# A hybrid decoder step: both roundings of a seam's bank ahead of its remainders, and a scheduler priority on one read of the decode's gates

## The chip, the cores and the metric

One core of a Trainium2 chip runs the kernel. The core has five engines with an instruction stream each: TensorE (PE, matmuls and transposes; its weight loads are shown apart as PEld), VectorE (DVE), ScalarE (ACT), GpSimd (POOL, which here mostly issues gathers) and SyncE (SP, which issues plain transfers). The metric is the device time of one execution in microseconds; the times shown are medians over several runs.

## The reference

One layer of a decoder, applied to a prompt of 1024 rows and to 8 decode sequences of one new row and 8192 cached rows each. All in fp32, D_MODEL 1024, D_FF 2816, 8 attention heads of 64, a paged key/value cache.

```
q, k, v, logf, u, z = mixer_inputs(rmsnorm(xp, g_mix), w_in, b_f, g_sgu_v)
xp = xp + merge_heads(fox_prompt(q, k, v, logf), sgu_prompt(u, z, w_s, b_s), g_att_out, g_sgu_out, w_o)
mk, mv = memory_kv(mem_prompt, g_mem, w_ck, w_cv)
xp = xp + cross_attend(rmsnorm(xp, g_cross), mk, mv, w_cq, w_co)
f, conv = conv_ffn(rmsnorm(xp, g_ffn), zeros, w_up, conv_w, conv_b, w_down)
xp = xp + f
...
def fox_attend(q, k, v, cq, ck, qpos, kpos):
    s = jnp.einsum('bqhd,bkhd->bhqk', q, k).astype(jnp.float32) * (ATT_HEAD_DIM ** -0.5)
    s = s + (cq... - ck...)
    p = jax.nn.softmax(where(kpos <= qpos, s, -inf), axis=-1)
    return jnp.einsum('bhqk,bkhd->bqhd', p, v)
```

The decode sequences go through the same steps with keys and values gathered by a page table; their attention over 8192 rows carries a forget gate, whose cumulated sum is subtracted from the scores.

## The kernel before

**Precision.** TensorE multiplies fp32 operands that have been rounded to a shorter form (fp32r). To keep fp32 accuracy each operand is split in two: the rounded value and the remainder. A product is then three matmuls: `gemm3` issues rounded x rounded (L272), rounded x remainder (L273) and remainder x rounded (L274); `gemm3_late` issues the same three in two sweeps (L280, L281, then L284). The helper `split` does the rounding on ScalarE (L235, or L238 where a gain is multiplied in) and the remainder on VectorE (L236, or L239). The remainder reads the rounded value, so L239 always waits for its L238. Weights are fetched in 128x1024 pieces by SyncE (names wr) and split as they come (wh and wl).

**Stages.** The prompt runs through input projection, attention, gating and output projection, and then, in two halves of 512 rows ("first half", "second half"), through cross-attention and the gated feed-forward network (FFN). The decode's attention runs beside all of that: its keys are gathered by GpSimd in pieces of 128x2048 (L1428), multiplied by the query on VectorE (L1444) and summed per head (L1448); after 16 pieces a softmax follows (L1460 and L1462, a transpose L1468, L1471 to L1474, L1481, the subtraction L1483, the exponent L1484 on ScalarE, the sum L1485); its values are gathered (L1489) into the same kind of buffer (kv) and multiplied on TensorE (L1495). The decode's instructions are put in as background work between the prompt's: `behind(e)` ties one to the newest instruction of engine e.

**The seams.** Between one stage of a half and the next stands a norm. `out_proj` adds to the rows (L1015), squares them (L230) and computes a factor per block of rows (L1031 on ScalarE, L1032 on GpSimd, a power); L1037 scales blocks 0 and 1, L1044 (ScalarE) and L1045 (VectorE) scale blocks 2 and 3 (y2, y3). `norm_T` then transposes the rows on TensorE (L1124), four 128x128 pieces to a bank of PSUM, with two row blocks (t0 = 0, then 2) and four banks for each; a bank holds two quarters of 128x256. For each quarter in turn it calls `split` with the norm's gain: ScalarE rounds (L238), VectorE takes the remainder (L239). `fill` (L1102) puts filler products ahead of the late transposes. `first` issues the products of the next stage's first outputs that need nothing more. `norm_T` runs four times: the cross seam and the FFN seam of the first half (about 521 to 548 us and 685 to 706 us in the profile), and those of the second (about 1154 to 1180 us and 1317 to 1337 us).

**The gates.** `gates` runs once for each of the 8 decode sequences. A small matmul (L1418) puts the sums of the gates into PSUM (ms), and one VectorE instruction (L1420) reads it and writes the decay per position (dec), which the softmax's first instruction (L1460) uses.

**What sets the order.** The program's text gives each instruction and its priority. The order on each engine is made at build time by a scheduler that simulates a timeline: at each point it takes the ready instruction of the best priority, by its own estimate of durations. Within `tc.high_priority()` an instruction gets precedence; `tc.issue_after(x)` makes it wait for x to be issued. At run time each engine then takes its instructions strictly in that order, so an instruction that waits holds up everything behind it. A change to a few lines can thus move instructions far away.

## Time and profile before

| | before |
|---|---|
| median of 3 runs | 1794.42 us (1788.66, 1794.93, 1794.42) |
| the profiled execution | 1793.69 us |
| its span, first to last instruction | 1791.7 us |
| mean granted TensorE clock | 0.993 |
| groups of L238 at the seams, 128x256 | 64 instructions, mean 475 to 477 ns |
| groups of L239 at the seams, 128x256 | 64 instructions, mean 473 ns |
| L1420 | 8 instructions, mean 1062 ns |

The profile is that of one execution. Its tables give the busy time of each engine; where an engine stood idle, the timeline shows in brackets how long, and the instruction whose end released it. "u" in these views is any operand buffer of the prompt (a rounded value, a remainder or a scaled row block), "ba" and "bb" are banks of PSUM, "kv" a decode buffer, "s" the decode's scores.

### The profile page before, as it was taken

To read this page: it belongs to the slowest core of one execution; us is meant where nothing else is said; L and a number is where in the kernel's file an instruction comes from. 1 tells how busy PE (TensorE), PEld (TensorE's weight loads), DVE (VectorE), ACT (ScalarE), POOL (GpSimd) and SP (SyncE) were. 2 spreads that over 40 slices of the span, in tenths; PEclk is the share of its full clock that TensorE was granted. 3 is DMA by queue.
4 is the path that set the end of the run, shared out by engine and by line. 5 is a ranking of instruction groups with operands and counts; after the bars stand their busy time and mean duration, and the time that the engine had idled before them with its cause. 6 is when DMAs were issued, how large, how long until landed. Compare 5 with 4: busy or idle time off the path is not lost.

```text
span 1791.7 us, 25124 instructions
## 1 busy us (share of the span) xinstructions
PE 1735.9 (97%) x9653; PEld 1285.7 (72%) x9653; DVE 1399.9 (78%) x1733; ACT 733.5 (41%) x1374; POOL 488.3 (27%) x461
## 2 busy tenths in 40 slices
PE   8999999889999999999999999999999999999997
PEld 5787777655677666767777777766666778768875
DVE  4689658989788986989999999898885549855344
ACT  6332355566643635333333244335353233333232
POOL 1252234443222332333322223433322112102110
PEclk9999999999999999999999999999999999999999
DMA  8786798777697975779788788988879587568982
GB/s 291 297 304 226 294 334 319 259 264 244 254 403 279 363 299 224 282 285 345 290 301 313 291 317 311 376 306 346 320 280 350 214 306 249 191 260 297 359 310 80
DMA packets 157074, 521.06 MB, mean 291 GB/s; under 512 B 20874, under 2 KB 40842, under 8 KB 124186
## 3 DMA queue, kind: packets, MB, share of 16 engines
q0 software_dynamic: 57168, 341.14, 50.0%
q1 hardware_dynamic: 92874, 165.73, 26.5%
q10 hardware_dynamic: 6912, 12.59, 1.9%
q8 instruction: 76, 1.25, 0.3%
q14 instruction: 44, 0.36, 0.1%
HBM read 495.47 MB, written 23.93 MB: 290 GB/s over the span
## 4 chain that ended last, share of the span: by engine, by line
PE 53%; issue 9%; DMA 8%; DVE 6%; ACT 2%; POOL 2%; POOLq 0%; DVEq 0%; ACTq 0%; SPq 0%
DMA kv<-cache_v,io 6%; PE ba L272 6%; PE ba L274 6%; PE ba L273 6%; PE dv L1495 4%; PE bb L272 3%; PE bb L273 3%; PE bb L274 3%; PE ba L1063 1%; DVE s L1448 1%; PE ba L1064 1%; PE ba L1065 1%; PE dv L331 1%; DMA kv<-cache_k,io 1%; PE dv L1774 1%
## 5 line engine op out<-in xcount | busy, mean ns | idle before, releaser
L235 ACT ACTIVATE wh<-wr 128x1024 fp32r<-128x1024 f32 (+2 forms) x220 | 228.6, 1044 | 443.3 <-PE ba L273 142.3
L236 DVE TENSOR_TENSOR wl<-wr,wh 128x1024 fp32r<-128x1024 f32 (+2 forms) x220 | 262.7, 1200 | 165.1 <-PE ba L274 57.4
L1428 POOL DMA_INDIRECT kv<-cache_k,io x128 | 186.9, 1460 | 606.8 <-DVE s L1448 327.2
L1444 DVE TENSOR_TENSOR kv<-kv,d 128x1024 f32<-128x1024 f32 (+1 forms) x156 | 258.0, 1681 | 32.6 <-DMA kv<-cache_k,io 32.6
L1448 DVE TENSOR_REDUCE s<-kv 128x16 f32<-128x1024 f32 (+1 forms) x156 | 258.4, 1672 | 0.0
L1489 POOL DMA_INDIRECT kv<-cache_v,io x128 | 160.8, 1256 | 239.4 <-PE dv L1495 155.2
L272 PE MATMUL ba<-u,wh 128*128 128x512 f32 x528 | 209.3, 397 | 0.0
L274 PE MATMUL ba<-u,wl 128*128 128x512 f32 x528 | 209.0, 396 | 0.0
L273 PE MATMUL ba<-u,wh 128*128 128x512 f32 x528 | 208.5, 395 | 0.5 <-DVE u L239 0.5
L272 PE MATMUL ba<-wh,u 128*128 128x512 f32 (+1 forms) x495 | 186.1, 379 | 0.9 <-ACT u L235 0.9
L273 PE MATMUL ba<-wl,u 128*128 128x512 f32 (+1 forms) x495 | 185.1, 375 | 1.3 <-DVE wl L236 1.3
L274 PE MATMUL ba<-wh,u 128*128 128x512 f32 (+1 forms) x495 | 183.4, 375 | 0.0
L1495 PE MATMUL dv<-kv,s 128*32 128x512 f32 x1024 | 127.1, 598 | 1.6 <-DMA kv<-cache_v,io 1.6
L274 PEld LDWEIGHTS ba<-u,wl 128*128 128x128 f32 x528 | 99.2, 188 | 29.0 <-issue 6.5
L272 PEld LDWEIGHTS ba<-u,wh 128*128 128x128 f32 x528 | 99.3, 188 | 26.4 <-issue 4.8
L273 PEld LDWEIGHTS ba<-u,wh 128*128 128x128 f32 x528 | 99.2, 188 | 25.2 <-issue 2.3
L272 PEld LDWEIGHTS ba<-wh,u 128*128 128x128 f32 x495 | 93.0, 188 | 25.0 <-issue 6.5
L272 PE MATMUL bb<-u,wh 128*128 128x512 f32 x272 | 108.7, 400 | 0.0
L274 PE MATMUL bb<-u,wl 128*128 128x512 f32 x272 | 108.0, 398 | 0.0
L273 PE MATMUL bb<-u,wh 128*128 128x512 f32 x272 | 107.9, 397 | 0.0
L273 PEld LDWEIGHTS ba<-wl,u 128*128 128x128 f32 x495 | 93.0, 188 | 20.1 <-DVE wl L236 1.9
L274 PEld LDWEIGHTS ba<-wh,u 128*128 128x128 f32 x495 | 92.9, 188 | 19.5 <-issue 1.6
(454 smaller groups left out, 3310.6 us busy)
## 6 DMA issues: line engine op xcount, KB each, us to landing
wr<-w_up SPq DMA_DIRECT2D x88, 512.0 KB
kv<-w_up POOLq DMA_DIRECT2D x22, 1024.0 KB
wr<-w_down SPq DMA_DIRECT2D x40, 512.0 KB
kv<-w_down POOLq DMA_DIRECT2D x11, 1024.0 KB
wr<-w_in SPq DMA_DIRECT2D x16, 512.0 KB
wr<-w_o SPq DMA_DIRECT2D x16, 512.0 KB
wr<-w_cq SPq DMA_DIRECT2D x16, 512.0 KB
wr<-w_co SPq DMA_DIRECT2D x16, 512.0 KB
```

Of the source, the lines that this page charges most:

```text
L235: nc.scalar.activation(h, src, AF.Copy)
L236: nc.vector.tensor_tensor(l, src, h.bitcast(F32), op=ALU.subtract)
L272: mmul(out, sh, mh, start=(i == 0), stop=False)
L273: mmul(out, sh, ml, start=False, stop=False)
L274: mmul(out, sl, mh, start=False, stop=(i == n - 1))
L331: mmul(ps[32 * j : 32 * j + 32, :w], xT[:, k, :] if nk == 8 else xT[:, k * 8 : k * 8 + 32], raw[:, q, j * w : (j + 1) * w], start=(k == 0) ...
L1063: mmul(pss[i], mh[k][:, tb], wh, start=(k == korder[0]), stop=False)
L1428: nc.gpsimd.indirect_dma_start(kv, None, a["cache_k"], off(kidx[:, b, ch : ch + 1]))
L1444: nc.vector.tensor_tensor(kvv[:, i : i + m, :], kvv[:, i : i + m, :], qb.unsqueeze(1).broadcast_to((P, m, 512)), op=ALU.mult)
L1448: nc.vector.tensor_reduce(s[:, ch * 4 + i : ch * 4 + i + m, :].rearrange("p k h -> p (k h)"), kvv[:, i : i + m, :].rearrange("p k (h d) -> ...
L1489: nc.gpsimd.indirect_dma_start(kv, None, a["cache_v"], off(kidx[:, b, ch : ch + 1]))
L1495: mmul(dv[32 * j : 32 * j + 32, :], s[:, ch * 4 : ch * 4 + 4, :].rearrange("p k h -> p (k h)"), kvv[:, j, :], start=(ch == 1), stop=(ch == ...
```

## The change

Two edits. In `norm_T` the call of `split` for each quarter becomes: both roundings of a bank first (the new L1130), then both remainders (the new L1132). The arithmetic is that of `split` with a gain. In `gates` the one VectorE read is put under `tc.high_priority()`. No instruction is added or left out; from the new lines on, numbers are 5 higher, and 6 higher behind L1420.

```diff
-                    for q in range(2):
-                        k = kk + q
-                        split(tr[:, q * 256 : (q + 1) * 256], hs[k][:, c], ls[k][:, c], scale=gp[:, g0 + k : g0 + k + 1])
+                    gain = [gp[:, g0 + k : g0 + k + 1] for k in (kk, kk + 1)]
+                    src = [tr[:, q * 256 : (q + 1) * 256] for q in range(2)]
+                    for q in range(2):
+                        nc.scalar.activation(hs[kk + q][:, c], src[q], AF.Copy, scale=gain[q])
+                    for q in range(2):
+                        nc.vector.scalar_tensor_tensor(
+                            ls[kk + q][:, c], src[q], gain[q], hs[kk + q][:, c].bitcast(F32), op0=ALU.mult, op1=ALU.subtract
+                        )
...
-            nc.vector.tensor_tensor(
-                dt_, ps[:, :8].unsqueeze(1).broadcast_to((P, 64, 8)), A.rearrange("p (h k) -> p k h", k=64), op=ALU.subtract
-            )
+            with tc.high_priority():
+                nc.vector.tensor_tensor(
+                    dt_, ps[:, :8].unsqueeze(1).broadcast_to((P, 64, 8)), A.rearrange("p (h k) -> p k h", k=64), op=ALU.subtract
+                )
```

The order on the engines is the same up to about 520 us of the profile of before and again from about 1463 us. Between them 237 pieces differ on TensorE, and there are moves on all engines. The priority alone accounts for one of them: VectorE's read dec_1245 (near 678 us) steps in between the two halves of a multiply that it followed. Three places follow.

ScalarE at the FFN seam of the first half, before. u_1266, u_1269, u_1272 and u_1275 are the rounded banks 1 to 4 of the first two row blocks, two quarters each; u_982 is row block 2, u_1278 is y2.

```order
L238 ACTIVATE u_1266_6305<-bb_1268_6307,gp_82 128x256
L238 ACTIVATE u_1269_6316<-ba_1271_6318,gp_82 128x256
L238 ACTIVATE u_1272_6327<-ba_1274_6329,gp_82 128x256
L235 ACTIVATE wh_1311_6576<-wr_1309_6573 128x1024
L238 ACTIVATE u_1266_6305<-bb_1268_6307,gp_82 128x256
L238 ACTIVATE u_1269_6316<-ba_1271_6318,gp_82 128x256
L235 ACTIVATE wh_1318_6630<-wr_1316_6627 128x1024
L238 ACTIVATE u_1272_6327<-ba_1274_6329,gp_82 128x256
L230 ACTIVATE junk_1255_6274,sqx_1193_5897<-u_982_4762 128x512
L238 ACTIVATE u_1275_6338<-bb_1277_6340,gp_82 128x256
L1031 ACTIVATE fac2_1257_6279<-sqx_1193_5897,part_1194_5898 128x1
L1044 ACTIVATE u_1278_6373<-u_982_4762,fac2_1257_6279 128x512 x2
```

The same place in the change:

```order
L1130 ACTIVATE u_1266_6305<-bb_1268_6307,gp_82 128x256 x2
L1130 ACTIVATE u_1269_6316<-ba_1271_6318,gp_82 128x256 x2
L1130 ACTIVATE u_1272_6327<-ba_1274_6329,gp_82 128x256 x2
L235 ACTIVATE wh_1311_6576<-wr_1309_6573 128x1024
L235 ACTIVATE wh_1318_6630<-wr_1316_6627 128x1024
L1130 ACTIVATE u_1275_6338<-bb_1277_6340,gp_82 128x256 x2
L230 ACTIVATE junk_1255_6274,sqx_1193_5897<-u_982_4762 128x512
L1031 ACTIVATE fac2_1257_6279<-sqx_1193_5897,part_1194_5898 128x1
L1044 ACTIVATE u_1278_6373<-u_982_4762,fac2_1257_6279 128x512 x2
```

The second roundings of banks 1 to 3 have moved ahead of the weights' roundings; both of bank 4 now stand ahead of the square L230, where before the first stood behind it and the second behind L1044 (beyond the rows shown).

VectorE at the cross seam of the second half, before. u_1874, u_1877, u_1880 and u_1883 are the remainders of banks 1 to 4 of the last two row blocks; kv_1816 is a decode piece.

```order
L1448 TENSOR_REDUCE s_1633_8615<-kv_1815_9600 128x16 x2
L239 SCALAR_TENSOR_TENSOR u_1874_9910<-ba_1885_9977,gp_82,u_1873_9909 128x256
L1444 TENSOR_TENSOR kv_1816_9650<-kv_1816_9650,d2_1632_8613 128x1024 x2
L239 SCALAR_TENSOR_TENSOR u_1877_9921<-bb_1886_9986,gp_82,u_1876_9920 128x256
L1020 TENSOR_TENSOR rq0_1889_10037<-sqx_1787_9485 128x4
L239 SCALAR_TENSOR_TENSOR u_1880_9932<-ba_1887_9995,gp_82,u_1879_9931 128x256
L239 SCALAR_TENSOR_TENSOR u_1883_9943<-ba_1888_10004,gp_82,u_1882_9942 128x256
L239 SCALAR_TENSOR_TENSOR u_1874_9910<-ba_1885_9977,gp_82,u_1873_9909 128x256
L1448 TENSOR_REDUCE s_1633_8615<-kv_1816_9650 128x16 x2
```

The same place in the change:

```order
L1450 TENSOR_TENSOR kv_1816_9650<-kv_1816_9650,d2_1632_8613 128x1024 x2
L1015 TENSOR_TENSOR u_1804_9517<-ba_1850_9801,u_1804_9517 128x512
L1454 TENSOR_REDUCE s_1633_8615<-kv_1815_9600 128x16
L1132 SCALAR_TENSOR_TENSOR u_1874_9910<-ba_1885_9977,gp_82,u_1873_9909 128x256 x2
L1132 SCALAR_TENSOR_TENSOR u_1877_9921<-bb_1886_9986,gp_82,u_1876_9920 128x256 x2
L1454 TENSOR_REDUCE s_1633_8615<-kv_1816_9650 128x16 x2
L1132 SCALAR_TENSOR_TENSOR u_1880_9932<-ba_1887_9995,gp_82,u_1879_9931 128x256 x2
L1132 SCALAR_TENSOR_TENSOR u_1883_9943<-ba_1888_10004,gp_82,u_1882_9942 128x256 x2
```

Both multiplies of kv_1816 have moved ahead of the first remainder of bank 1 and ahead of the addition L1015; its sums stand between banks 2 and 3.

TensorE in the FFN of the first half, before. The two L1495 rows (4 matmuls each) are the first pair of V products of the decode sequence whose scores are s_1022; ba, bb, wh and u are the FFN's.

```order
L272 MATMUL bb_1367_6943<-u_1269_6316,wh_1366_6940 128x512
L1495 MATMUL dv_1322_6668<-kv_1324_6670,s_1022_5011 32x512 x4
L1495 MATMUL dv_1322_6668<-kv_1323_6669,s_1022_5011 32x512 x4
L273 MATMUL bb_1367_6943<-u_1270_6317,wh_1366_6940 128x512
L274 MATMUL bb_1367_6943<-u_1269_6316,wl_1365_6939 128x512
```

In the change:

```order
L272 MATMUL ba_1385_7075<-wh_1377_6994,u_1330_6711 128x512
L273 MATMUL ba_1385_7075<-wl_1376_6993,u_1330_6711 128x512
L1501 MATMUL dv_1322_6668<-kv_1324_6670,s_1022_5011 32x512 x4
L1501 MATMUL dv_1322_6668<-kv_1323_6669,s_1022_5011 32x512 x4
L272 MATMUL ba_1398_7121<-wh_1391_7106,u_1298_6520 128x512
```

The pair stands 57 rows later, in the down projection instead of the up projection. The second pair (kv_1349 and kv_1350) moves 41 rows, from 3126 to 3167 of TensorE's order, so 27 rows lie between the starts of the pairs where 43 lay. On ScalarE the exponent of s_1022 moves from ahead of the rounding of wh_1391 to behind that of wh_1397, and on VectorE the subtraction L1483 and the sum L1485 of s_1022 stand behind several remainders of weights that they preceded.

## The prediction

> **What bounds the kernel now.** I read the page first (busy shares, slices, chain), then who waits for the split's instructions, then the timelines of the engines at the four seams, and last the stretch where the order moves most.
>
> ```profile
> PE 1735.9 (97%) x9653; PEld 1285.7 (72%) x9653; DVE 1399.9 (78%) x1733; ACT 733.5 (41%) x1374; POOL 488.3 (27%) x461
> PE   8999999889999999999999999999999999999997
> DVE  4689658989788986989999999898885549855344
> PE 53%; issue 9%; DMA 8%; DVE 6%; ACT 2%; POOL 2%; POOLq 0%; DVEq 0%; ACTq 0%; SPq 0%
> ```
>
> The span is 1791.7 us, so TensorE is idle for 1791.7 - 1735.9 = 55.8 us in all. No reordering that leaves the matmuls as they are can win more than that, and a seam can only give back the wait that stands in front of a matmul there. VectorE is the second bound: its slices 17 to 25 of 40 (717 to 1120 us) stand at 8 and 9. What is late in that stretch has little room to catch up.
>
> Who waited for the rounding (the call in L1129, whose two instructions are L238 on ScalarE and L239 on VectorE):
>
> ```profile
>   DVE u L239: 13.2, 8
>   PEld ba L280: 3.1, 5
>   PEld bb L280: 2.2, 2
>   PE bb L280: 1.7, 1
>   PE ba L280: 1.2, 3
> ```
>
> VectorE lost 13.2 us to it and TensorE 1.7 + 1.2 = 2.9; the weight loads' idle time lies beside TensorE's. A saving on VectorE is a saving of the kernel only where TensorE waits behind it.
>
> **The change, part by part.** It adds and removes no instruction: 64 roundings and 64 remainders of 128x256 remain, at 475 and 473 ns each by their groups. What changes is (a) the order written in a bank, (b) a priority on eight reads, and (c) what the scheduler makes of both on every engine from about 520 us on.
>
> *The priority (b).*
>
> ```profile
> L1420 DVE TENSOR_TENSOR dec<-ms,d x8: 1021/1063/1084, 150.4 to 1286.2; 128x512 f32<-128x512 f32 x8
>   PE ms L852: 2.7, 1
> ```
>
> Only one of the eight reads moves: dec_1245 steps ahead of one half of a kv multiply near 678 us. The one time that TensorE waited for such a read (2.7 us) is at 315 us, ahead of the first moved instruction. Nobody waits at 678; the multiply behind it (128x1024, 1218 ns by its group) is 1.06 us later on VectorE. If TensorE did wait for what that multiply feeds, it would cost 1.06 us; by the row I take 0.
>
> *Cross seam of the first half.* Here TensorE has no idle time to return:
>
> ```profile
> 521.00:548.00 27.00, 27.00 (x163) 20.64 (x163) 26.10 (x37) 12.89 (x27) 5.18 (x5) 1.00 0.94 344
> ```
>
> Gain 0. Loss: other decode work covers the remainders; without that cover one bank would cost two remainders, 0.95 us. I take 0.
>
> *FFN seam of the first half.*
>
> ```profile
> 694.00 0.39 PE L280 MATMUL ba<-u,wh 128*128 128x256 f32 x1 [0.32 <-ACT u L238]
> 695.51 0.38 PE L280 MATMUL ba<-u,wh 128*128 128x256 f32 x1 [0.57 <-DVE u L239]
> 697.71 0.33 PE L1124 MATMUL bb<-cp,u 128*128 128x128 f32 x1 [1.70 <-ACT u L1044]
> 698.68 0.39 PE L280 MATMUL ba<-u,wh 128*128 128x256 f32 x1 [0.64 <-ACT u L238]
> 704.00 0.27 PE L1124 MATMUL ba<-cp,u 128*128 128x128 f32 x1
> 696.32 1.33 ACT L1044 ACTIVATE u<-u,fac 128x512 f32<-128x512 f32 x2 [0.68 <-POOL fac L1032]
> 698.17 0.45 ACT L238 ACTIVATE u<-bb,gp 128x256 fp32r<-128x256 f32 x1
> 698.66 0.48 DVE L239 SCALAR_TENSOR_TENSOR u<-bb,gp,u 128x256 fp32r<-128x256 f32 x1 [2.69 <-ACT u L238]
> 699.47 0.88 DVE L1045 TENSOR_SCALAR u<-u,fac 128x512 f32<-128x512 f32 x2 [0.33 <-POOL fac L1032]
> ```
>
> The fourth bank's second rounding stood behind the scaling of y2 (L1044) and came at 698.17; now it follows the first at about 695.4. The waits of 0.32, 0.57 and 0.64 go. In exchange two roundings stand ahead of the square (L230) that starts the chain square, factor, power on GpSimd, scaling: L1044 begins about 1.0 us later (697.4) and y3 (L1045) at 699.47 + 1.0 = 700.5. TensorE now has the bank's products behind it and waits for y3 instead; the last transpose follows the end of y3's second half (700.5 + 0.88 = 701.4) by about eight transposes of 0.12 us, so it ends near 702.4 where it began at 704.00 before. That gives 1.6 us. Bounds: nothing, if y3 is later still; 3.2 us, the sum of the four waits, if the scaling is not delayed. I take -1.6.
>
> The clock is part of that place:
>
> ```profile
> 694.00:698.00 4.00, 1.73 (x9) 1.14 (x9) 1.97 (x5) 2.89 (x7) 0.57 (x1) 1.00 1.00 420
> 699.40:703.00 3.60, 3.60 (x20) 3.60 (x19) 2.41 (x7) 0.75 (x3) 1.04 (x2) 0.53 0.67 278
> ```
>
> After 4 us in which TensorE was busy for 1.73, it ran at 0.53 for 3.6 us, which costs 3.60 x 0.47 = 1.7 us. Those filler products (L1102) lie ahead of the transposes that set the end, so the dip is inside the 1.6 us, not added to it. The Trainium skill, "TensorE: Matmul & The Clock Gate", section "Part 1: The HAM clock gate (the "warmup" mystery)", says that the clock falls to half after an idle window of about 3.4 us. The longest gap here is 1.70 us, so the trace disagrees: scattered waits were enough. By the page no dip would come with or without the change and the seam's sum would hold only the waits; by the row a denser seam may keep the clock, and a longer wait for y3 may lose it.
>
> *Decode work behind that seam (706 to 810 us).* This is the largest move. The softmax of the running decode sequence (subtraction L1483, exponent L1484, sum L1485) comes 12 to 20 us later in VectorE's and ScalarE's order, weight remainders (L236) come earlier, and the first pair of V products on s_1022 stands 57 TensorE rows later.
>
> ```profile
> L1495 PE MATMUL dv<-kv,s x32: 592/592/617, 769.4 to 783.6; 128*32 128x512 f32 x32
> 778.73 0.39 PE L273 MATMUL ba<-wl,u 128*128 128x512 f32 x1
> 780.57 0.40 PE L273 MATMUL bb<-wl,u 128*128 128x512 f32 x1
> 782.27 1.06 PE L1495 MATMUL dv<-kv,s 128*32 128x512 f32 x8 [1.31 <-DMA kv<-cache_v,io]
> 770.78 0.94 POOL L1489 DMA_INDIRECT kv<-cache_v,io  x1 [11.38 <-PE dv L1495]
> 772.02 4.86 POOL L1489 DMA_INDIRECT kv<-cache_v,io  x1 [0.30 <-issue]
> 777.18 2.14 POOL L1428 DMA_INDIRECT kv<-cache_k,io  x1 [0.30 <-issue]
> 787.47 2.29 DVE L1444 TENSOR_TENSOR kv<-kv,d 128x2048 f32<-128x2048 f32 x1 [4.25 <-DMA kv<-cache_k,io]
> 787.90 1.06 ACT L235 ACTIVATE wh<-wr 128x1024 fp32r<-128x1024 f32 x1 [4.01 <-PE ba L274]
> 757.00:805.00 48.00, 46.69 (x225) 33.95 (x225) 43.28 (x42) 15.91 (x24) 16.23 (x10) 1.00 0.80 284
> ```
>
> Eight matmuls take 780.57 - 778.73 = 1.84 us, 0.23 each. The first pair moves by 57 x 0.23 = 13.1 us, from 769.4 to 782.5. The exponent now stands behind the rounding of wh_1397, which waited for TensorE until 787.90 and is released earlier in the new order; I give it 0.4 us of wait. This pair releases the buffers of the next two V gathers: before, the gather was issued 1.4 us after the pair began, the second 1.24 later, and it was used 782.27 - 772.02 = 10.25 us after its issue. Now that makes 782.9 + 1.4 + 1.24 + 10.25 = 795.8. TensorE arrives at the second pair sooner than before: 27 rows lie between the pairs' starts, not 43, 25 of them matmuls: 25 x 0.23 plus 1.85 for the first pair is 7.7 us, so 782.9 + 7.7 = 790.6. The wait becomes 5.2 us by this gather and about 2.5 if the transfer needs 7.5; against 1.31 before it is 1.2 to 3.9 more, and I take +3. The K gather of kv_1356 is queued behind the two on GpSimd, so VectorE's multiply, which waited 4.25 us for it before, starts near 797 to 801, with the split of an FFN operand (u_1358) behind it on VectorE. That operand was ready at 801.1 and would be at 800 to 804, against a TensorE that is itself 3 us late: 0 to 3, and I take +1. Together +4. It is hidden entirely if the gathers land in 4 us, which no gather here does.
>
> The same kind of move at 1040 to 1100 us has no TensorE wait for a gather in the trace of before: 0, with 2 either way.
>
> *Cross seam of the second half.*
>
> ```profile
> 1176.35 0.50 PE L273 MATMUL ba<-u,wh 128*128 128x512 f32 x1 [0.47 <-DVE u L239]
> 1179.52 0.39 PE L280 MATMUL bb<-u,wh 128*128 128x256 f32 x1 [1.70 <-ACT u L238]
> 1176.21 2.35 DVE L1444 TENSOR_TENSOR kv<-kv,d 128x1024 f32<-128x1024 f32 x2
> 1178.49 0.47 DVE L239 SCALAR_TENSOR_TENSOR u<-bb,gp,u 128x256 fp32r<-128x256 f32 x1
> ```
>
> ScalarE's second rounding waited for VectorE's remainder of the first half, which was queued behind two kv multiplies; TensorE waited 1.70 us for it. Both roundings now come first, so this wait goes. The multiplies now stand ahead of all remainders of this bank, and TensorE needs those too, a few products later: I leave 0.9 of the 2.17 us standing. -1.3, between -2.2 and +1.2 (one multiply more on the path).
>
> *FFN seam of the second half.*
>
> ```profile
> 1326.43 0.39 PE L280 MATMUL ba<-u,wh 128*128 128x256 f32 x1 [1.05 <-DVE u L239]
> 1330.61 0.33 PE L1124 MATMUL ba<-cp,u 128*128 128x128 f32 x1 [0.77 <-ACT u L1044]
> 1329.84 1.34 ACT L1044 ACTIVATE u<-u,fac 128x512 f32<-128x512 f32 x2 [0.68 <-POOL fac L1032]
> ```
>
> The 1.05 us goes, but y2 at 1329.84 sets the end and its chain is as long as before: what is saved first is waited for there. 0, from -1.1 to +0.5.
>
> Sum: -1.6 + 4 - 1.3 = +1.1 us on the profiled 1793.69, which is 0.7 below the median of the runs: 1794.8, so 1795.
>
> **The rivals.**
>
> *Slower: the gathers fall behind and stay there.* Place: 782 to 890 us. The V pair waits 5.2 us, the K multiply adds 3, and because VectorE is nearly full the next three V pairs wait again, by an estimate half of what the first adds, 2 us each: 3.9 + 3 + 6 = 13 us, less 2.9 at the seams: 1804. It decides if gathers take 10 us or more from issue to use while VectorE has nothing else to do. For it: the 4.86 us that one gather held its queue, and the 4.25 and 1.31 us waits that exist already. Against it: TensorE's own delay hands the same time to all that follows, and VectorE had 4.7 us of idle time between 757 and 805.
>
> *Faster: the seams give everything.* 3.23 at the first FFN seam, 2.17 and 1.82 at the second half's, 1.7 of clock, and the decode's move hidden: 8.9, so 1785. For it: all those waits are in front of TensorE. Against: y2 and y3 follow a chain of their own on three engines, and the decode's V gathers wait for a pair that surely comes later.
>
> *The change does nothing measurable:* the scheduler's new order only permutes waits; 1794. It lies inside my forecast's own range.
>
> **How the numbers follow.** About 0.5%, 9 us, is what a measurement of this kernel can tell from no change. Forecast, with its own range 1788 to 1801 from the bounds of the terms: 0.52 (the do-nothing case included). Slower rival 0.29, faster rival 0.19. The bounds for 0.5% are 1785.4 and 1803.4 around the median; the two rivals' times lie at these edges, so their chances stand for the outer sides, and I give faster 0.19, same 0.52, slower 0.29. The range reaches to the faster rival with 2 us beyond it and to the slower rival with a fourth late pair and more: 1783 to 1812.
>
> **What would show it.** Right: no TensorE wait on the rounding or remainder above 0.6 us near 694 to 699, 1176 to 1180 and 1326; the last transpose of the first FFN seam near 702.4; a TensorE wait for cache_v of 2.5 to 5.2 us near 790; the same time to 520 us. Wrong: V waits repeated through 890, a long VectorE wait for cache_k with TensorE idle behind it, a clock below 1 for longer than 3.6 us, or a seam whose TensorE idle time grew because remainders now come later.

## The result, and the profile after

| | before | the change |
|---|---|---|
| median | 1793.35 us (6 runs, 1788.66 to 1795.85) | 1803.33 us (6 runs, 1801.81 to 1806.05) |
| ratio to before | 1 | 1.0058, 95% interval 1.0042 to 1.0073 |
| profiled execution | 1793.69 us | 1801.81 us |
| its span | 1791.7 us | 1800.0 us |

The change is slower by 0.58%, 10 us. That lies inside the range of the prediction, and just beyond the 0.5% that it called the limit of a measurement, on the slower side. The forecast of 1795 was 8 us too low.

The page of the profile after, its busy times and its chain of waits:

```profile
PE 1735.3 (96%) x9653; PEld 1284.7 (71%) x9653; DVE 1398.9 (78%) x1733; ACT 731.7 (41%) x1374; POOL 505.9 (28%) x461
PE 56%; DVE 8%; issue 8%; DMA 6%; POOL 2%; ACT 1%; POOLq 0%; DVEq 0%; SPq 0%; ACTq 0%
```

TensorE worked 1735.3 us, VectorE 1398.9 and ScalarE 731.7, each within 2 us of before. What grew is TensorE's idle time: 1800.0 - 1735.3 = 64.7 us, where it was 55.8. One other number moved: GpSimd, which here mostly issues gathers, was busy for 505.9 us and not 488.3. The gathers held their queue 17.6 us longer in all.

TensorE's waits after, by the instruction that ended them (total, times, longest). These are the main rows above 1 us that before did not have, or had with a shorter longest wait:

```profile
PE dv L1501 <- DMA kv<-cache_v,io: 4.9, 1, 4.9
PE ba L1193 <- ACT t L1180: 4.5, 3, 3.3
PE bb L1193 <- ACT t L1180: 1.7, 1, 1.7
PE ba L280 <- DVE u L1132: 1.3, 1, 1.3
PE ba L1124 <- DVE u L1045: 1.2, 1, 1.2
PE bb L1124 <- DVE u L1045: 1.2, 1, 1.2
```

(Two more rows grew in the same way: the wait for u L1214 from 1.0 to 1.4 us at its longest, and a new one of 1.4 us for u L1345, below.) Before, no wait on cache_v was above 1.31 us. The three largest are not at an instruction of a seam. The first stands at 1244 us, the next two rows' longest at 616 and 603 us, in the cross-attention of each half; before's own longest in the second of these rows was 1.23 us, at 617. Only the last three rows are at a seam, the FFN seams.

To see where time was gained and lost, each TensorE instruction of a run was set against the same instruction of the profile of before. The table shows how many us later it starts (a median over those around each place); the last column is taken at 1780 us.

| us of before's profile | 515 | 638 | 703 | 812 | 1150 | 1236 | 1310 | 1358 | end |
|---|---|---|---|---|---|---|---|---|---|
| the change | -3.1 | +0.4 | -2.0 | -1.3 | +0.1 | -3.1 | +3.5 | +7.9 | +8.3 |
| the change again (e12) | -3.3 | +3.3 | +0.9 | -0.2 | +2.9 | +2.4 | +9.8 | +9.9 | +10.2 |
| before with the priority alone (e1) | -4.0 | -3.5 | -2.7 | -2.9 | -3.1 | -3.1 | +2.0 | +0.3 | +0.4 |
| all but the last seam (e2) | -4.0 | -0.5 | -2.9 | -1.3 | +1.7 | -1.4 | +5.6 | +6.1 | +7.2 |
| first cross seam alone (e4) | -3.9 | +1.5 | +2.1 | +2.5 | +2.4 | +4.0 | +9.2 | +7.3 | +7.3 |
| the change, more filler at the last seam (e7) | -2.9 | +0.7 | -1.7 | -1.6 | -0.1 | -3.3 | -1.5 | -0.6 | +0.2 |
| the change, four remainders tied (e9) | -4.0 | +2.7 | +0.3 | -0.6 | +0.6 | -2.5 | +0.5 | -1.9 | -0.9 |

Two things limit what it can tell. Up to 515 us the order of all engines is the same in every row, and yet the executions differ by 4 us: a step of 4 us in one profile is no finding by itself. And e1, whose times equal before's, lost 5.1 us between 1236 and 1310 where the profile of before lost none; e4, which has before's order there, lost 5.2. So a step counts here only where several executions of one order show it and those of the other order don't.

One does, plainly: from 515 to 638 us, the cross seam of the first half and the attention behind it. All six profiles with the new order there lost 3.5 to 6.7 us; the seven others (e1, e3, e5, e6, e8, e10, e11) moved by -0.1 to +0.6. The second, less sharp, is the stretch from 1236 to 1358 us: 11.0 and 7.5 us lost by the change and 7.5 by e2, against 3.4 by e1 and 3.3 by e4.

**The loss at 1244 us.** What VectorE, GpSimd and SyncE did before the wait, and what TensorE met, in the change (start, duration, in brackets the idle time and what ended it):

```profile
1231.17 2.34 DVE L236 TENSOR_TENSOR wl<-wr,wh 128x1024 fp32r<-128x1024 f32 x2
1232.12 5.62 POOL L1495 DMA_INDIRECT kv<-cache_v,io  x1 [1.39 <-PE dv L1501]
1232.47 1.44 SPq L249 DMA_DIRECT2D wr<-w_co  x2
1233.42 2.36 DVE L1450 TENSOR_TENSOR kv<-kv,d 128x1024 f32<-128x1024 f32 x2
1235.69 1.22 DVE L236 TENSOR_TENSOR wl<-wr,wh 128x1024 fp32r<-128x1024 f32 x1
1238.05 0.96 POOL L1495 DMA_INDIRECT kv<-cache_v,io  x1 [0.30 <-issue]
1249.02 3.53 PE L1501 MATMUL dv<-kv,s 128*32 128x512 f32 x16 [4.94 <-DMA kv<-cache_v,io]
```

The same place before:

```profile
1231.59 2.35 DVE L1444 TENSOR_TENSOR kv<-kv,d 128x1024 f32<-128x1024 f32 x2
1232.88 1.88 POOL L1489 DMA_INDIRECT kv<-cache_v,io  x1 [4.18 <-PE dv L1495]
1233.85 1.22 DVE L236 TENSOR_TENSOR wl<-wr,wh 128x1024 fp32r<-128x1024 f32 x1
1234.99 1.21 DVE L1448 TENSOR_REDUCE s<-kv 128x16 f32<-128x1024 f32 x1
1235.06 0.94 POOL L1489 DMA_INDIRECT kv<-cache_v,io  x1 [0.30 <-issue]
1235.14 0.37 SPq L249 DMA_DIRECT2D wr<-w_co  x1
1239.58 3.49 DVE L236 TENSOR_TENSOR wl<-wr,wh 128x1024 fp32r<-128x1024 f32 x3
```

Before, VectorE took one remainder of an output weight (w_co) at 1233.85, then a sum (L1448), and three more remainders at 1239.58. In the change two remainders, two multiplies and a third remainder stand back to back from 1231.17 to 1236.91. The first V gather was issued into this run at 1232.12 and held GpSimd's queue for 5.62 us, until 1237.74. The second could only be issued at 1238.05, 3 us later than before, and TensorE stands for 4.94 us.

What held the first gather? Two things differ from before. Each remainder frees the buffer of a raw weight, and SyncE at once loads the next one into it: before, one w_co load went out at 1235.14, behind both V gathers; in the change two went out at 1232.47, 0.35 us behind the first gather, with o_mk and o_mv behind them. And VectorE's run is longer. The profiles tell the two apart. In e1, which has before's order, a K gather in the same stretch held the queue even longer, with no load issued in the 3 us behind it:

```profile
1234.20 2.35 DVE L1445 TENSOR_TENSOR kv<-kv,d 128x1024 f32<-128x1024 f32 x2
1234.56 6.22 POOL L1429 DMA_INDIRECT kv<-cache_k,io  x1 [1.66 <-DVE s L1449]
1236.47 3.50 DVE L236 TENSOR_TENSOR wl<-wr,wh 128x1024 fp32r<-128x1024 f32 x3
1239.87 2.35 DVE L1449 TENSOR_REDUCE s<-kv 128x16 f32<-128x1024 f32 x2
```

VectorE's run of multiplies and remainders ended at 1239.97 and the gather at 1240.78; in the change the run ended at 1236.91 and the gather at 1237.74, each time 0.8 us behind it. In the fourteen profiles 28 gathers of keys or values held the queue for over 4.5 us. Every one was issued during an unbroken run of VectorE instructions that take two operands from SBUF, the memory of all tiles that are not banks of PSUM (the remainders of weights and the decode's multiplies above all), and ended 0.82 to 0.83 us behind the run, before rounding; behind only four of the 28 had SyncE issued a load within 1 us. A sum, which takes one operand, ends such a run. So what the change did here is to put more of these instructions in a row. This is read from the profiles; no version changes VectorE's run alone. The loads have a smaller part: from the end of its issue the second V gather took 10.0 us to land in e2, with such loads ahead of it, and 8.1 in e9, with them behind it.

The wait costs more than its length. TensorE's clock in the microseconds behind it, in the change:

```profile
1250.00:1251.00 1.00, 1.00 (x8) 0.21 (x4) 0.00 (x0) 0.00 (x0) 0.00 (x0) 0.50 0.19 76
```

The 16 V products took 3.53 us at half clock; a pair without a wait takes 1.92 (at 789.64, below). That is another 1.6 us, so about 6.5 at the spot (e7, below, gives what it costs in the end).

**The loss at 603 to 619 us.** GpSimd, VectorE and TensorE in the change; cmx is the maximum of the cross-attention's softmax, t an operand that ScalarE copies:

```profile
603.23 3.94 POOL L1434 DMA_INDIRECT kv<-cache_k,io  x1 [4.05 <-DVE s L1454]
614.14 2.36 DVE L1450 TENSOR_TENSOR kv<-kv,d 128x1024 f32<-128x1024 f32 x2 [2.66 <-DMA kv<-cache_k,io]
616.42 0.69 DVE L1195 TENSOR_REDUCE cmx<-ba 128x2 f32<-128x512 f32 x1
619.19 3.72 PE L1193 MATMUL ba<-t,u 128*128 128x256 f32 x16 [3.31 <-ACT t L1180]
```

The same in e1, which has before's order and reached this place with the same lead:

```profile
599.86 1.67 POOL L1429 DMA_INDIRECT kv<-cache_k,io  x1 [1.67 <-DVE s L1449]
609.17 2.35 DVE L1445 TENSOR_TENSOR kv<-kv,d 128x1024 f32<-128x1024 f32 x2
611.44 0.68 DVE L1190 TENSOR_REDUCE cmx<-ba 128x2 f32<-128x512 f32 x1
614.22 3.72 PE L1188 MATMUL ba<-t,u 128*128 128x256 f32 x16 [0.57 <-ACT t L1175]
```

The order inside these 20 us is the same in both. Only the K gather is late: issued 3.37 us later, and holding its queue for 3.94 us and not 1.67. VectorE's multiply waits 2.66 us for it, and the softmax's maximum, queued behind that multiply, comes 5 us later, then two steps of ScalarE (L1198 at 617.14, L1180 at 618.55), then TensorE. The 3.94 us are of the same kind as the 5.62 above: the gather was issued into a multiply and two remainders that ended at 606.36, again 0.8 us before it did. So the new order acts at a distance: the orders differ only ahead of this stretch, from 521 us on, where VectorE's decode work sets when GpSimd may gather. One link was seen there: the K gather at 568.27 us met two multiplies and two remainders in a row and held its queue for 5.09 us in the change, and the one at 570.12 us met no such run and held it for 0.94 in e1. The links between were not followed one by one. e1's wait of 0.57 us is at the low end: in the profiles with before's order at this seam it lies between 0.56 and 1.72 us.

### The profile page after: what moved, and what is told of

The parts are those of the page before. It is cut to its first block, busy times and chain, and to the rows that moved or that the text cites. A ratio compares the mean times of both kernels' runs of the same rounds, so it can differ in the third digit from the quotient of the medians.

```text
span 1800.0 us, 25148 instructions
## 1 busy us (share of the span) xinstructions
PE 1735.3 (96%) x9653; PEld 1284.7 (71%) x9653; DVE 1398.9 (78%) x1733; ACT 731.7 (41%) x1374; POOL 505.9 (28%) x461
## 4 chain that ended last, share of the span: by engine, by line
PE 56%; DVE 8%; issue 8%; DMA 6%; POOL 2%; ACT 1%; POOLq 0%; DVEq 0%; SPq 0%; ACTq 0%
PE ba L272 8%; PE ba L274 8%; PE ba L273 8%; PE bb L272 4%; PE bb L274 4%; PE bb L273 4%; PE dv L1501 4%; DMA kv<-cache_v,io 3%; DMA kv<-cache_k,io 2%; DVE kv L1450 1%; PE dv L331 1%; DVE s L1454 1%; PE dv L1780 1%; PE ba L1063 1%; PE ba L1064 1%
## 5 line engine op out<-in xcount | busy, mean ns | idle before, releaser
L1434 POOL DMA_INDIRECT kv<-cache_k,io x128 | 197.7, 1545 | 577.1 <-DVE s L1454 327.1
L1454 DVE TENSOR_REDUCE s<-kv 128x16 f32<-128x1024 f32 (+1 forms) x156 | 258.5, 1673 | 0.0
L1495 POOL DMA_INDIRECT kv<-cache_v,io x128 | 167.6, 1310 | 261.6 <-PE dv L1501 151.3
```

What stands on the lines that cost most here:

```text
L1434: nc.gpsimd.indirect_dma_start(kv, None, a["cache_k"], off(kidx[:, b, ch : ch + 1]))
L1454: nc.vector.tensor_reduce(s[:, ch * 4 + i : ch * 4 + i + m, :].rearrange("p k h -> p (k h)"), kvv[:, i : i + m, :].rearrange("p k (h d) -> ...
L1495: nc.gpsimd.indirect_dma_start(kv, None, a["cache_v"], off(kidx[:, b, ch : ch + 1]))
```

## The experiments

A counter in `norm_T` numbers the seams in the order of their calls: 0 and 1 are the cross and the FFN seam of the first half, 2 and 3 those of the second. Most versions keep the change's text and take the old `split` in the other seams:

```diff
+        seam = seams[0]
+        seams[0] += 1
...
-                    for q in range(2):
-                        nc.scalar.activation(hs[kk + q][:, c], src[q], AF.Copy, scale=gain[q])
-                    for q in range(2):
-                        nc.vector.scalar_tensor_tensor(
-                            ls[kk + q][:, c], src[q], gain[q], hs[kk + q][:, c].bitcast(F32), op0=ALU.mult, op1=ALU.subtract
-                        )
+                    if seam in (0, 1, 2):
+                        for q in range(2):
+                            nc.scalar.activation(hs[kk + q][:, c], src[q], AF.Copy, scale=gain[q])
+                        for q in range(2):
+                            nc.vector.scalar_tensor_tensor(
+                                ls[kk + q][:, c], src[q], gain[q], hs[kk + q][:, c].bitcast(F32), op0=ALU.mult, op1=ALU.subtract
+                            )
+                    else:
+                        for q in range(2):
+                            split(src[q], hs[kk + q][:, c], ls[kk + q][:, c], scale=gain[q])
```

Shown is e2; of the others only the line with the seams is given below. The priority of the change stays in all of them. All were timed beside before on the same chip, whose median was 1793.3 to 1793.6 us. The ratio is not the quotient of the two medians; where the two disagree, the interval decides.

| | version | median us | ratio to before, 95% interval |
|---|---|---|---|
| e1 | the priority alone | 1794.40 | 1.0004 [0.998, 1.0028] |
| e2 | seams 0, 1, 2 | 1800.11 | 1.0028 [1.0012, 1.0044] |
| e3 | seam 3 alone | 1793.60 | 1.0003 [0.9988, 1.0018] |
| e4 | seam 0 alone | 1795.59 | 1.0009 [0.9995, 1.0024] |
| e5 | seam 1 alone | 1795.30 | 1.0012 [0.9996, 1.0029] |
| e6 | seam 2 alone | 1793.47 | 1.0004 [0.9984, 1.0024] |
| e7 | the change, 16 filler products at the last seam | 1802.62 | 1.0062 [1.0037, 1.0086] |
| e8 | seams 1, 2 | 1796.31 | 1.0029 [1.0015, 1.0043] |
| e9 | the change, four weight remainders tied | 1792.40 | 0.9995 [0.9979, 1.0012] |
| e10 | seams 1, 2, tied the same way | 1793.09 | 0.9993 [0.9975, 1.001] |
| e11 | seam 1, tied the same way | 1797.54 | 1.002 [1.0002, 1.0037] |
| e12 | the change again | 1802.85 | 1.0046 [1.003, 1.0062] |

**e1: the priority alone.** Before's `norm_T` stays; in `gates`:

```diff
+            with tc.high_priority():
                 nc.vector.tensor_tensor(
```

> The kernel before with the priority on the gates' read alone. Theory (the priority moves one VectorE instruction near 678 us that nobody waits for): within 2 us of the kernel before, 1793; no new TensorE wait. Rival (the read's place costs TensorE its 1.06 us or more in the following seam): 1 to 3 us slower, and a TensorE wait near 690 us that the kernel before lacks. As a second look at an almost unchanged order it also shows how far the part up to 515 us drifts by chance (3.1 us between the two profiles so far).

1794.40 us, no difference. The priority is not part of the loss, and what follows is about the seams. Its profile serves as a second one of before's order.

**e2 and e3: the last seam taken out, and alone.**

e2 is the diff above. e3, against it:

```diff
-                    if seam in (0, 1, 2):
+                    if seam in (3,):
```

> The whole change, but the FFN seam of the second half keeps the old order in a bank; the engines' order is that of the change up to about 1317 us and that of the kernel before from about 1340 us. Theory (that seam alone costs 4.4 us, of 7.9 lost between 640 us and the end): 4 us faster than the change, about 3.5 slower than before, 1797; the TensorE waits of 1.30, 0.61, 0.98 and 1.19 us there shrink to those of before (1.05, 0.77, 0.51) and the clock stays at 1.00. Rival (the seam is late because the decode work ahead of it is late, whatever the order in the bank): as slow as the change, 1803, with the clock again at half for some us.

> The kernel before with the priority, and the new order in a bank at the FFN seam of the second half alone; the order differs from before only from 1317 to about 1400 us. Theory (this seam's remainders come late on VectorE, TensorE idles and the clock falls to half): 4 us slower than before, 1797 to 1798, remainders ended about 3 us later than the roundings' ends allow, clock 0.5 for some 6 us. Rival (it takes the earlier shifts as well): within 1 us of before.

Without its last seam the change takes 1800.11 us, about 3 less than with it, though the two intervals overlap. The last seam alone costs nothing: 1793.60. So its price is not its own; it is paid only where the rest has the new order too. Most of the loss, 7 of 10 us, stands without it, and the waits at 616 and 1244 us are both in e2's profile (the second with 5.03 us).

**e4: the first cross seam alone.**

```diff
-                    if seam in (0, 1, 2):
+                    if seam in (0,):
```

> The kernel before with the priority, and the new order at the cross seam of the first half alone; the order differs from before from 515 to 598 us only. Theory (the 3.4 us that TensorE lost at 603 to 620 us in the profile of the change were a lead by chance, given back to a chain that the gathers and VectorE pace): within 1 us of before. Rival (the seam's new order delays the cross-attention's exponent): 3 us slower, with TensorE waits of 1.7 and 3.3 us for the exponent near 603 and 616 us even where the profile has no lead at 515 us.

TensorE in its profile:

```profile
604.67 1.99 PE L1201 MATMUL bb<-t,u 128*128 128x256 f32 x8 [1.70 <-ACT t L1188]
618.54 5.41 PE L1201 MATMUL ba<-t,u 128*128 128x256 f32 x16 [3.35 <-ACT t L1188]
```

Both waits are there again, as they are in all six profiles with this seam's new order (1.66 to 1.70 and 3.25 to 4.01 us), with the 16 products behind the second at 5.41 us and not 3.72. So this seam's order causes them. Of the two readings, that a chance lead is given back or that new waits appear, the trace shows the second. In the table above e4 loses 5.4 us between 515 and 638. By its time, though, e4 is only 2 us above before, with an interval that holds no change. Its profiled execution, of 1801.02 us, is the slowest of its ten (the fastest took 1793.30), so the profile shows more loss than the usual execution has; what makes up the rest of the difference wasn't found.

**e5, e6, e8: the middle seams, alone and together.**

```diff
-                    if seam in (0, 1, 2):
+                    if seam in (1,):
```

and in the same line `(2,)` for e6 and `(1, 2)` for e8.

> The kernel before with the priority, and the new order in a bank at the FFN seam of the first half alone; the order differs from before from 685 us to about 1400 us, and from the change at the second half's seams. In its order VectorE takes the remainder of the second w_co piece behind a decode multiply again, where the change has it 3.5 us earlier. Theory (that seam gains 2.5 us; the 4.9 us wait for a V gather near 1244 us comes from w_co and memory loads that the earlier remainders set free, 0.35 us behind the first of the two gathers): 2 to 4 us faster than before, 1790, and no TensorE wait for cache_v above 2 us near 1244. Rival (the shift of the decode by the seam makes that gather late by itself): 2 us slower than before, with the wait of some 5 us as in the change.

> The kernel before with the priority, and the new order in a bank at the cross seam of the second half alone. In its order VectorE takes three w_co remainders in a row, ahead of the decode multiplies, so the loads behind them are set free even sooner than in the change. Theory (the seam gains 2 to 3 us, and the loads that are set free get ahead of a V gather): gain at 1180 us, loss of 4 to 5 us near 1244 us with a TensorE wait for cache_v, in sum 1 to 3 us slower, 1795. Rival (the decode's shift from the FFN seam of the first half is needed for that wait): no such wait, 2 us faster than before, 1791.

> The new order at the FFN seam of the first half and the cross seam of the second, with the priority; the order is that of the change from 598 to 1317 us and that of before elsewhere. Theory (the places add up: first FFN seam -2.5, 703 to 1154 us +2, cross seam -3, V gather near 1244 us +4, and the cross seam of the first half not there): within 2 us of before, 1793 to 1795, and 3 to 5 us faster than the version that also has the first cross seam, with the wait of 5 us near 1244 us still there. Rival (the first cross seam's cost is given back later, so leaving it out gains nothing): 1799 to 1800.

Alone neither can be told from no change. Together they cost 3.0 us by the medians against the before of their chip; e2, which has seam 0 besides, costs 6.6 against its own. By the medians the first cross seam would thus be worth 3.6 us when the others are in; by the ratios, 1.0028 for e2 and 1.0029 for e8, it would be worth nothing. Its price in combination is not shown. The gather at 1244 shows that its wait needs no seam in particular, only an order with a long run of VectorE at that place: e5 waited 3.10 us for cache_v there, e8 5.82, and e6 not at all, though it waited 3.86 us for another V gather at 1318. None of the three was expected in just this form. The times of e8 lie at 1795.3 to 1796.4 us in six executions and at 1800.5 to 1801.4 in four; its profile, with the wait of 5.82 us, is one of the lower six, so this wait is not what divides them.

**e7: more filler at the last seam.** In the profile of the change the clock fell to half behind the last seam, and eight filler products more were to keep it up:

```diff
-    def fill(tr, hs):
+    def fill(tr, hs, n=8):
-        for k in range(8):
+        for k in range(n):
-                    fill(tr, hs)
+                    fill(tr, hs, 16 if seams[0] == 4 else 8)
```

> The whole change, with 16 filler products of L1102 instead of 8 at the FFN seam of the second half; the order is that of the change up to 1340 us but for the eight. They take 1.1 us and lie in the 0.98 us wait for y2. Theory (TensorE's idle time at this seam lets the clock fall to half for 6 us, 3 us of the seam's 4.4): the clock stays at 1.00 or falls for less than 3 us, 1800 to 1801, 2 to 3 us faster than the change. Rival (the clock falls for what comes later, the 1.19 us wait for y3, or by the chip's own measure): the same dip, 1803 to 1804. If the waits alone make the loss, there is no gain either.

1802.62 us, so nothing is won. Its profiled execution is worth more than the experiment: at 1793.71 us it is 8 us or more below each of the other four (1801.84 to 1807.19), and it has the order of the change up to the last seam. GpSimd and TensorE in it, at the place of the lost 4.94 us:

```profile
1231.95 1.08 POOL L1498 DMA_INDIRECT kv<-cache_v,io  x1 [1.39 <-PE dv L1504]
1233.34 1.97 POOL L1498 DMA_INDIRECT kv<-cache_v,io  x1 [0.30 <-issue]
1245.33 1.92 PE L1504 MATMUL dv<-kv,s 128*32 128x512 f32 x16
```

The first gather was through its queue in 1.08 us, although SyncE issued the same two loads 0.36 us behind it (1232.31) and VectorE had the same run of remainders and multiplies (from 1231.02 on). It slipped in between the first two remainders: it ended 0.8 us behind the first. The second went out at 1233.34, and TensorE waited for nothing. Up to 1236 us e7 and the change agree within 0.3 us in the table; at 1310 us they are 5.0 apart. So this gather's wait with its slow clock costs some 5 us, and whether it comes is settled in a fraction of a microsecond.

**e12: the change again**, with no edit.

> The change itself once more, on the chip of the runs beside it. Theory: 1802 to 1804, 0.5 to 0.6% slower than before; the waits for the exponent near 603 and 616 us of 1.7 and 3.3 us and the wait for cache_v near 1244 us are there again. Open is whether the clock falls to half at the last seam again: if the dip belongs to this order, it is there; if it comes by the position of a window, it may be missing.

1802.85 us, and waits of 1.67, 3.61 and 4.98 us at the three places: they belong to the order, not to one execution. The clock behind the last seam does not. The change:

```profile
1338.00:1342.00 4.00, 3.00 (x15) 3.00 (x15) 2.63 (x6) 2.05 (x7) 0.43 (x1) 0.50 0.87 364
```

and e12, which comes to the same work some 4.5 us later:

```profile
1342.00:1346.00 4.00, 2.66 (x21) 2.42 (x22) 2.96 (x8) 2.60 (x8) 0.54 (x1) 1.00 0.94 395
```

With the same waits of TensorE for y2 and y3 (0.98 and 1.19 us in the change, 0.97 and 1.19 here), one execution ran at 0.50 and the other at 1.00. They did not come to the seam quite alike: the change had waited 1.30 us for a remainder at 1330 us, and e12 had no such wait.

**e9: the change with four weight remainders tied.** The first four w_co weights of the second half may be split only after two given decode multiplies, so that VectorE takes their remainders where it took them before. All four seams keep the new order. The first added line stands behind each kv multiply in the decode.

```diff
+                multiplied.append(newest(ENG.DVE))
...
-                ws[kk] = wload(wpair(w, kk, n * 512, 512), 1024)
+                tied = ys is not None and seams[0] == 3 and n == 0
+                with tc.issue_after(multiplied[-8 if kk == 0 else -7]) if tied else nullcontext():
+                    ws[kk] = wload(wpair(w, kk, n * 512, 512), 1024)
```

> The whole change, with VectorE's remainders of the first four w_co pieces of the second half tied behind the decode's multiplies that they follow in the kernel before; up to 1230 us the order is that of the change, and at 1230 to 1243 us VectorE's weight remainders stand as before. Theory (the early remainders set free two w_co loads and two memory loads, 1.5 MB, that are issued 0.3 us behind the first gather of a V pair and ahead of the second, which then comes 5 us late): the loads start about 3 us later, both gathers stand ahead of them, no TensorE wait for cache_v above 1 us near 1244 us, 4 to 5 us faster than the change, 1798 to 1799. Rival (the gather is late because the decode reaches it sooner after its buffer is free): the wait of some 5 us stays, and the time is that of the change, 1803.

Its engines at the place:

```profile
1232.67 1.06 POOL L1503 DMA_INDIRECT kv<-cache_v,io  x1 [1.39 <-PE dv L1509]
1233.96 1.23 DVE L236 TENSOR_TENSOR wl<-wr,wh 128x1024 fp32r<-128x1024 f32 x1
1234.04 1.97 POOL L1503 DMA_INDIRECT kv<-cache_v,io  x1 [0.30 <-issue]
1235.28 0.37 SPq L249 DMA_DIRECT2D wr<-w_co  x1
1239.77 2.35 DVE L236 TENSOR_TENSOR wl<-wr,wh 128x1024 fp32r<-128x1024 f32 x2
```

One remainder at 1233.96, the others from 1239.77, the load at 1235.28 behind both gathers: the picture of before. With a sum behind the one remainder (at 1235.18), VectorE's run is short again. The wait for cache_v is gone, and the time is 1792.40 us, 10.5 below the change beside it on the same chip. That is more than the 5 that the wait is worth. From 1236 to 1358 us e9 loses 0.6 us, against 11.0 and 7.5 in the two profiles of the change. The tie also changed the order at the last seam, where its only wait is of 0.54 us, so a part of the gain lies there: of what e9 is better by behind 1236 us, 3.6 us lie before 1310 and 6.8 behind it against the one profile of the change, 4.4 and 2.5 against the other. It still pays at the first cross seam, with a wait of 4.01 us at 615. And the tie moves VectorE's run and SyncE's loads together, so by itself it does not say which of the two mattered.

**e10 and e11: the same tie with fewer seams.** e10 is e8 with the tie, e11 is e5 with it.

> The middle seams' version (new order at the first FFN seam and the second cross seam, priority) with the same tie. If the places add up: -2.5 at the first FFN seam, +2 up to 1154 us, -3 at the second cross seam, and nothing at 1244 us: 1790 to 1792, 2 us faster than before. Rival (what the tie saves comes back as another wait before 1320 us): 1795 to 1797, as the middle seams without it.

> The new order at the FFN seam of the first half alone, with the same tie. Its profile without the tie has a TensorE wait of 3.1 us for cache_v near 1249 us. Theory: that wait falls below 1 us, and the version comes out 1 to 3 us faster than without the tie, 1792 to 1794. Rival: the wait stays, 1795.

e10 takes 1793.09 us, 0.5 below before, where e8 without the tie was 3.0 above its own; the interval doesn't tell it from no change. In e11 the wait for cache_v fell from 3.10 to 0.77 us, as it should, and the time did not follow: 1797.54, with 3.13 us of wait on ScalarE at 1257 where e5 had 1.02 (e1 and e4 had 2.73 there, without any tie). So removing this wait pays in some orders and not in all. Both also bear on what holds a gather: their loads follow the first V gather by 2.6 and 2.7 us, and still it held the queue for 3.34 us in e10 and 3.50 in e11, until 0.8 us behind VectorE's two multiplies and one remainder. No version is faster than before by more than its interval.

## Where the prediction was right and where it failed, point by point

The measured time lies in the stated range, and that owes something to the range's width of 29 us: the sum's largest term did not come as described, and the places where most of the time was lost had a 0 or no term. Its terms, with the steps of the two profiles of the change in the table above:

| step | predicted us | the change | again (e12) |
|---|---|---|---|
| to 515 us | 0 | -3.1 | -3.3 |
| cross seam, first half, and the attention behind it (to 638) | 0 | +3.5 | +6.6 |
| FFN seam, first half (to 703) | -1.6 | -2.4 | -2.4 |
| decode behind it (to 812) | +4 | +0.7 | -1.1 |
| 812 to 1150 | 0 | +1.4 | +3.1 |
| cross seam, second half (to 1236) | -1.3 | -3.2 | -0.5 |
| 1236 to 1310 | no term | +6.6 | +7.4 |
| FFN seam, second half (to 1358) | 0 | +4.4 | +0.1 |
| to the end | 0 | +0.4 | +0.3 |
| sum | +1.1 | +8.3 | +10.2 |

**The FFN seam of the first half: right.** TensorE's transposes and products there, after:

```profile
695.36 0.39 PE L280 MATMUL ba<-u,wh 128*128 128x256 f32 x1 [0.56 <-ACT u L1130]
698.07 0.33 PE L1124 MATMUL ba<-cp,u 128*128 128x128 f32 x1 [0.75 <-ACT u L1044]
700.77 0.88 PE L1124 MATMUL ba<-cp,u 128*128 128x128 f32 x6 [1.21 <-DVE u L1045]
702.03 0.27 PE L1124 MATMUL ba<-cp,u 128*128 128x128 f32 x1
```

The waits of 0.32, 0.57, 0.64 and 1.70 us have become 0.56, 0.75 and 1.21; TensorE waits for y3, as forecast, and the last transpose starts at 702.03. The prediction gave 702.4 for its end, and set that against its start of 704.00 before; start against start, the gain is 2.0 us. These waits sum to 2.52 us where they were 3.23. The rest of the 2.4 us gained goes with the clock, which the prediction had left inside its 1.6:

```profile
698.00:702.00 4.00, 2.72 (x22) 2.49 (x23) 0.96 (x3) 3.30 (x11) 1.27 (x2) 1.00 1.02 422
```

It stays at 1.00 where it had fallen to 0.53 for 3.6 us.

**The cross seam of the second half: right in kind, sized too small.** Neither the 1.70 nor the 0.47 us of wait is left; the largest between 1150 and 1235 us is 0.45. The gain is 3.2 us in the change and 3.1 to 3.2 in e2, e7 and e9, where 1.3 was forecast and 2.2 was the bound; in e12 it is 0.5.

**The decode behind the first FFN seam: mis-sized, by a wrong step.** GpSimd's gathers, VectorE's multiply and TensorE, after:

```profile
773.42 1.80 POOL L1495 DMA_INDIRECT kv<-cache_v,io  x1 [16.88 <-DVE s L1454]
779.26 0.94 POOL L1495 DMA_INDIRECT kv<-cache_v,io  x1 [4.04 <-DVE s L1454]
781.82 1.92 PE L1501 MATMUL dv<-kv,s 128*32 128x512 f32 x16 [0.54 <-ACT s L1490]
789.64 1.92 PE L1501 MATMUL dv<-kv,s 128*32 128x512 f32 x16
793.15 2.29 DVE L1450 TENSOR_TENSOR kv<-kv,d 128x2048 f32<-128x2048 f32 x1 [6.50 <-DMA kv<-cache_k,io]
802.23 0.50 PE L272 MATMUL ba<-wh,u 128*128 128x512 f32 x1 [1.44 <-DVE u L1345]
```

The pair came at 781.82 with 0.54 us of wait for the exponent, and the second at 789.64, both as worked out (782.9 with 0.4, and 790.6). But "this pair releases the buffers of the next two V gathers" no longer held: both were issued before the pair, released by the sums of keys (L1454). So the wait of 2.5 to 5.2 us never came. The late K gather did: 6.50 us of wait on VectorE, and 1.44 on TensorE where +1 was taken. A buffer's next user has to be looked up in the new order too; the old owner was carried over.

**The cross seam of the first half: "I take 0" failed.** The argument was that TensorE was busy for all of 521 to 548 us. That is true after, too (26.85 of 27 us), and says nothing on what the seam's reordering hands on. The price in these profiles, 3.5 to 6.6 us, falls 55 to 70 us later, in a stretch whose own order did not change. The prediction named the cover ("other decode work covers the remainders") and did not ask what becomes of the decode work that gives the cover: it moves later, and with it the gathers that it releases.

**1236 to 1310 us: a term that was missing.** The moves of weight remainders at that place were in the order, but none of the places that were costed. The slower rival had the right kind of mechanism, gathers that fall behind, and nearly the right time (1804); it put it at 782 to 890 us and made GpSimd late through the V pair. The prediction had seen that a gather held its queue for 4.86 us (at 772 us, before) and did not ask what held it. It was a run of VectorE, as at 1232 us in the change. Remainders moved together there make the run longer, and one V gather then comes 3 us late; the loads that they set free come early as well, with the smaller part. That the place of four remainders decides the loss is shown by e9: its ten times, 1791.0 to 1797.2 us, all lie below those of the change beside it, 1801.6 to 1805.2. That VectorE's run, more than the loads, is the link is read from the profiles of e1, e7, e10 and e11, and of the 28 long gathers.

**The FFN seam of the second half: 0 was nearly right by its waits** (0.1 us in e12), and 4.4 where the clock fell. "The 1.05 us goes" held in e12; in the change 1.30 us of wait for a remainder stood there, where the prediction's sign of being right was none above 0.6. By the times of e2 and of the change it costs 3 us in combination and, by e3, nothing alone. Why, is open.

**What stays open.** The profiles place 7.5 to 11 us of the loss between 1236 and 1358, against 3.4 in e1 and none in the profile of before; some 5 of it is the gather with its slow clock. The first cross seam shows a loss of 3.5 to 6.7 us in every profile that has it, and by the times some 2 us alone and 0 to 3.6 in combination, neither told from nothing. These prices do not add up exactly, since each execution differs by some 4 us before the first moved instruction and the waits come in most executions and not in all. Why e9 wins 10.5 us and not 5 is settled only in part.

## What to carry to other kernels

When an order changes, look not only at who waits for the moved instruction but at what else the engine's new sequence holds up: here VectorE instructions moved together kept GpSimd from issuing a gather, by up to 5 us. Look also at which buffers are set free and on which queue the next load stands ready, since work done earlier starts transfers earlier. Cost a seam to the end of the stage behind it, not to the seam's own end. And take several profiles of the kernel before, because one profile's waits are partly chance.

## What the runs showed of the hardware

A gather's issue holds GpSimd's queue for 0.94 us in the quiet case, and for 5.62, 5.61, 5.62 and 5.60 us in the four versions where TensorE then waited about 5 us or more at 1244 us (the change, e12, e2, e8). In each, SyncE issued two loads of 512 KB 0.29 to 0.35 us behind the gather, but that is not what its length follows: in e7 the same loads followed by 0.36 us and the gather took 1.08; in e1 and e4 a gather took 6.22 us with no load in the 3 us behind it. It follows VectorE. All 28 gathers of keys and values above 4.5 us, in all fourteen profiles, ended 0.82 to 0.83 us behind the end of an unbroken run of VectorE instructions with two operands in SBUF. Such a run does not hold every gather that is issued into it: the one in e7 got in between two of its instructions. Which gathers get in is open.

A wait of a few microseconds is followed by half clock, but not always. TensorE at 616 us in e12, whose wait of 3.61 us is only 0.30 longer than the one quoted of the change:

```profile
619.38 6.40 PE L1193 MATMUL ba<-t,u 128*128 128x256 f32 x16 [3.61 <-ACT t L1180]
```

The same 16 products took 6.40 us here and 3.72 in the change. So 3 us of the difference between the two executions are 0.3 us of wait and 2.7 of clock. The Trainium skill, "TensorE: Matmul & The Clock Gate", section "Part 1: The HAM clock gate (the "warmup" mystery)", gives an idle window of about 3.4 us that runs freely, so that its place against the work is chance. The waits of 3.31 us, with a full clock behind it, and of 3.61 and 4.94 us agree with that. Three things do not: the half clock behind the last seam in the change, where the longest gap was 1.30 us (e12, with 1.19 us as its longest there, kept the full clock); e4, where the 16 products behind a wait of 3.35 us took 5.41 us, while those behind 3.38 us in e7 took 3.72; and e1, where after a wait of 2.73 us at 1260 us the clock was 0.54 and two products took 2.08 us that take 1.13 elsewhere. A wait well under the page's window can cost clock, and a slightly longer one may cost none.
